# The low parts of the down-projection weights made by an accumulating DMA instead of by VectorE

## The chip, the cores and the metric

One core of one Trainium2 chip runs the whole program in one launch. The metric is the device time of that core in microseconds (us), lower is better. Times are medians of several executions; the profile is of one execution.

## What is computed

The reference is a decoder trunk of two layers in float32 on 256 tokens of width 1024. The part that matters here is the feed-forward block, which stands twice in every layer (four times in the run), before and after a group of token mixers:

```python
D_MODEL, SEQ, DEPTH, D_FF = 1024, 256, 2, 2816

def swiglu(x, w_up, w_down):
    g, u = jnp.split(x @ w_up, 2, axis=-1)
    return (jax.nn.silu(g) * u) @ w_down

for i in range(DEPTH):
    x = x + 0.5 * swiglu(rmsnorm(x, norm_ffn1[i]), w_ffn1_up[i], w_ffn1_down[i])
    ...
    x = x + 0.5 * swiglu(rmsnorm(x, norm_ffn2[i]), w_ffn2_up[i], w_ffn2_down[i])
    ...
```

The mixers (windowed attention, a gated recurrence, latent attention, each with its projections) and the per-layer embedding gate are left out here; the change does not touch them.

## The kernel before, in words

**Three products for one.** TensorE is fed float32r operands (a float32 rounded to fewer mantissa bits). To keep float32 accuracy, each operand is split into a rounded part h and a remainder l = value - h, and `mm3` (lines 205 to 209) adds three matmuls: h times h (L207), h times the low part of the moving operand (L208) and the low part of the stationary operand times h (L209). In the down projection the weights are the moving operand, so L208 is the matmul that reads a weight's l.

**Units.** Weights come in units of up to 128 partitions x 1024 elements (512 KB). `fetch` (lines 187 to 193) takes a `raw` tile and has SyncE (SP) load it from HBM. `split_unit` (lines 195 to 203) takes an `h` and an `l` tile, has ScalarE (ACT) write h as a rounding copy of raw (L201) and VectorE (DVE) write l = raw - h (L202). `unit` (lines 182 to 185) does both. There are 4 buffers for raw, 5 for h and 5 for l (line 1056); a buffer is taken again when all readers of its last content are done. So the load of a unit waits, at the head of SP's queue, for the DVE subtraction four units earlier, and the ACT copy of a unit waits for the matmuls of the unit five earlier. The whole run has 512 units; 88 of them, all 128x1024, are of the down projections.

**The feed-forward block** (`ffn`, lines 288 to 374) runs over 11 blocks of 256 hidden columns. Block b takes four up units, runs 16 matmul triples with them into two PSUM tiles (one for each half of the tokens), has ACT apply silu (L308) and DVE the product (L309), and then runs the down projection of the block before it, with two down units d0 and d1, each of 128 hidden rows x 1024 columns. In program order a block's units are thus u0, u1, u2, u3, d0, d1. In blocks 1 to 9 the up units are consumed one after the other, for both token halves; in the first and the last block token half by token half, so that there the four units come free only in the second pass.

**The last block** (lines 353 to 373) runs two down projections: d0 and d1 of block 9, then d0 and d1 of block 10, with the norm of the finished token half after them. Four down units are alive at once.

**Order on the engines.** The order of the instructions on each engine is laid down when the program is built and follows program order by priority, with waits on semaphores; each engine and each DMA queue takes its instructions in that order. GpSimd (POOL) has little to do: the power for the norms (L224), a product (L589), and two DMA issues at the start (L960, L971).

Of the kernel before, what the change touches and what calls it, by code (L numbers as in the profile page):

```python
# [9 lines left out]
F32R = mybir.dt.float32r  # L10
BF16 = mybir.dt.bfloat16
I32 = mybir.dt.int32
AF = mybir.ActivationFunctionType
OP = mybir.AluOpType
# [115 lines left out]
class Build:  # L130
# [51 lines left out]
    def unit(self, name, block, q):  # L182
        if (name, block, q) in self.early:
            return self.early.pop((name, block, q))
        return self.split_unit(*self.fetch(name, block, q))

    def fetch(self, name, block, q):
        nc = self.nc
        off, k, n = self.where[self.layer][name, block, q]
        m = k * n  # L190
        raw = self.wraw.tile([128, 1024], F32, name="raw")
        nc.sync.dma_start(raw[:, :m], self.a[f"weights{self.layer}"][off:off + 128 * m].rearrange("(p m) -> p m", p=128))
        return raw, k, n
# [908 lines left out]
```

## Time and profile before

| what | us |
|---|---|
| median of 2 runs | 1562.87 |
| the runs | 1562.22, 1563.51 |
| span of the profiled execution | 1560.1 |
| busy in it: PE, PEld, DVE, ACT, POOL | 1538.6, 1285.2, 940.4, 867.1, 36.4 |

PE is TensorE's matmuls, PEld its weight loads (they overlap), DVE is VectorE, ACT ScalarE, POOL GpSimd, SP SyncE. The span runs from the first to the last instruction of the profiled execution; the 2.8 us between it and the median is what lies around the span and the scatter of the runs. Matmuls are pipelined and their ends are modelled: a matmul of 512 columns is shown with some 0.39 us, but the next one starts about 0.23 us after it.

### The profile page before, as it was taken

The numbers are of one execution on the slowest core, as the hardware profiler recorded it, in microseconds if no ns is written. First come the engines' busy times: TensorE is split into PE (matmuls) and PEld (weight loads), VectorE is DVE, ScalarE is ACT, GpSimd is POOL, SyncE is SP. The second block draws the span as 40 slices with busy tenths as digits, with TensorE's granted clock in tenths as the row PEclk, the third lists the DMA queues.
The fourth block names the chain that finished last, engine by engine and source line by source line (L and its number), as shares of the span: only waits on it lengthen the run. The fifth ranks groups of instructions, "written<-read, shape, count | busy, mean of one in ns | idle before, by whom it ended". The sixth has DMA issues, their size and how long they took to land.

```text
span 1560.1 us, 20882 instructions
## 1 busy us (share of the span) xinstructions
PE 1538.6 (99%) x7896; PEld 1285.2 (82%) x7896; DVE 940.4 (60%) x1504; ACT 867.1 (56%) x1315; POOL 36.4 (2%) x48
## 2 busy tenths in 40 slices
PE   8999999999999999999999999999999999999997
PEld 6888888899878888888888888889998788888886
DVE  6555577567756665555765456675677466655456
ACT  6444486477564464444764445855875644644455
POOL 0000010000000000000000000100000000000000
PEclk9999999999999999999999999999999999999999
DMA  8555545343425555565565554544335355556652
GB/s 303 187 191 187 172 156 176 125 146 130 156 88 182 189 183 188 177 193 173 180 202 189 176 192 158 181 150 137 125 110 176 116 195 177 188 189 188 188 171 95
DMA packets 76469, 264.61 MB, mean 170 GB/s; under 512 B 8608, under 2 KB 9520, under 8 KB 76368
## 3 DMA queue, kind: packets, MB, share of 16 engines
q1 hardware_dynamic: 76144, 263.06, 51.5%
q8 instruction: 62, 1.02, 0.3%
q0 software_dynamic: 80, 0.16, 0.1%
q14 instruction: 39, 0.32, 0.1%
q10 hardware_dynamic: 144, 0.05, 0.0%
HBM read 262.19 MB, written 1.05 MB: 169 GB/s over the span
## 4 chain that ended last, share of the span: by engine, by line
PE 94%; ACT 2%; DVE 2%; DMA 1%; issue 1%; POOL 0%; SPq 0%; POOLq 0%; DVEq 0%; ACTq 0%
PE pu L207 21%; PE pu L209 21%; PE pu L208 21%; PE acc L207 5%; PE acc L208 5%; PE acc L209 5%; PE sq L209 2%; PE sq L208 2%; PE sq L207 2%; PE psa L497 1%; PE pt L314 1%; PE pt L234 1%; PE po L519 1%; PE psc L841 1%; DMA raw<-in_weights_dram 1%; PE psc L840 1%
## 5 line engine op out<-in xcount | busy, mean ns | idle before, releaser
L202 DVE TENSOR_TENSOR l<-raw,h 128x1024 fp32r<-128x1024 f32 (+3 forms) x512 | 599.9, 1185 | 399.2 <-ACT h L201 394.0
L201 ACT CAST h<-raw 128x1024 fp32r<-128x1024 f32 (+1 forms) x511 | 512.0, 1016 | 380.4 <-PE pu L209 236.6
L207 PE MATMUL pu<-h,xth 128*128 128x512 f32 (+3 forms) x1376 | 534.3, 389 | 7.1 <-DVE h L201 6.4
L208 PE MATMUL pu<-l,xth 128*128 128x512 f32 (+3 forms) x1376 | 525.5, 382 | 2.1 <-DVE l L202 2.1
L209 PE MATMUL pu<-h,xtl 128*128 128x512 f32 (+3 forms) x1376 | 524.5, 381 | 0.0
L207 PEld LDWEIGHTS pu<-h,xth 128*128 128x128 f32 x1376 | 259.4, 189 | 52.7 <-ACT xth L217 6.3
L208 PEld LDWEIGHTS pu<-l,xth 128*128 128x128 f32 x1376 | 259.6, 189 | 48.5 <-DVE l L202 4.8
L209 PEld LDWEIGHTS pu<-h,xtl 128*128 128x128 f32 x1376 | 259.1, 188 | 46.7 <-issue 1.3
L207 PE MATMUL acc<-h,fh 128*128 128x512 f32 x352 | 140.2, 398 | 0.0
L209 PE MATMUL acc<-h,fl 128*128 128x512 f32 x352 | 139.1, 395 | 0.0
L208 PE MATMUL acc<-l,fh 128*128 128x512 f32 x352 | 138.9, 395 | 0.0
L209 PEld LDWEIGHTS acc<-h,fl 128*128 128x128 f32 x352 | 66.3, 188 | 15.5
L208 PEld LDWEIGHTS acc<-l,fh 128*128 128x128 f32 x352 | 66.5, 189 | 15.0
L207 PEld LDWEIGHTS acc<-h,fh 128*128 128x128 f32 x352 | 66.3, 188 | 14.6
L308 ACT ACTIVATE sg<-pu,rstd 128x256 f32<-128x256 f32 x88 | 41.8, 475 | 64.3 <-PE pu L209 64.2
L309 DVE SCALAR_TENSOR_TENSOR hd<-pu,rstd,sg 128x256 f32<-128x256 f32 x88 | 42.3, 480 | 39.0 <-ACT sg L308 39.0
L207 PE MATMUL pu<-h,fh 128*128 128x512 f32 x128 | 51.3, 401 | 1.6 <-DVE merged L896 1.6
L208 PE MATMUL pu<-l,fh 128*128 128x512 f32 x128 | 51.0, 398 | 0.0
L209 PE MATMUL pu<-h,fl 128*128 128x512 f32 x128 | 50.8, 397 | 0.0
L207 PE MATMUL sq<-h,xth 128*128 128x512 f32 x128 | 50.4, 394 | 0.0
L209 PE MATMUL sq<-h,xtl 128*128 128x512 f32 x128 | 50.1, 391 | 0.0
L208 PE MATMUL sq<-l,xth 128*128 128x512 f32 x128 | 50.1, 391 | 0.0
(230 smaller groups left out, 1411.1 us busy)
## 6 DMA issues: line engine op xcount, KB each, us to landing
raw<-in_weights_dram SPq DMA_DIRECT2D x446, 512.0 KB, 4.2
raw<-in_weights_dram SPq DMA_DIRECT2D x48, 384.0 KB, 3.4
raw<-in_weights_dram SPq DMA_DIRECT2D x8, 320.0 KB, 3.1
raw<-in_weights_dram SPq DMA_DIRECT2D x8, 256.0 KB, 2.7
xin<-in_xt_dram SPq DMA_DIRECT2D x4, 256.0 KB, 6.2
x<-in_x_dram SPq DMA_DIRECT2D x2, 512.0 KB, 8.9
out_dram<-o SPq DMA_DIRECT2D x4, 256.0 KB, 2.1
cf<-in_const_f_dram SPq DMA_DIRECT2D x1, 928.0 KB, 8.3
```

The source lines that it names most:

```text
L201: (copy or nc.scalar.copy)(h[:, :m], raw[:, :m])
L202: nc.vector.tensor_tensor(l[:, :m], raw[:, :m], h[:, :m].bitcast(F32), op=OP.subtract)
L207: mm(out, ah, bh, start=start, stop=False)
L208: mm(out, ah, bl, start=False, stop=False)
L209: mm(out, al, bh, start=False, stop=stop)
L234: nc.tensor.transpose(pt[:, k, :], src[:, half * 512 + k * 128:half * 512 + (k + 1) * 128], self.ident)
L308: nc.scalar.activation(sg, pu[t][:, 0, :], AF.Silu, scale=rstd[t])
L309: nc.vector.scalar_tensor_tensor(hd, pu[t][:, 1, :], rstd[t], sg, op0=OP.mult, op1=OP.mult)
L314: nc.tensor.transpose(pt[:, f, t * 128:(t + 1) * 128], hd[:, f * 128:(f + 1) * 128], self.ident)
L497: mm(ps[:, g, :], self.aqk[r, h // 2, qt * 128:(qt + 1) * 128], self.aqk[r, 6 + h // 2, kb * 128:(kb + 1) * 128], start=True, stop=True)
L519: mm(po[:, qt, :], PTt[n][:, g, :], self.av[:, kb, h * 64:(h + 1) * 64], start=(g == 0 and n < 2), stop=(g == 2 and n != 1))
L840: mm(o, qnT[:, hd, qt * 128:(qt + 1) * 128], knT[:, hd, 0:128 * (qt + 1)], start=True, stop=False)
```

## The change

For units whose name ends in `_down`, l is made in another way. ACT first writes l as the rounded copy of -raw, which is -h, and then h as before; then GpSimd issues a DMA from raw onto l that adds raw to what is there. The result, raw - h, is the same. The DVE subtraction of these units is gone. All other units are as before.

```diff
     def unit(self, name, block, q):
         if (name, block, q) in self.early:
             return self.early.pop((name, block, q))
+        if name.endswith("_down"):
+            return self.split_unit_by_dma(*self.fetch(name, block, q))
         return self.split_unit(*self.fetch(name, block, q))
+
+    def split_unit_by_dma(self, raw, k, n):
+        nc = self.nc
+        m = k * n
+        h = self.wh.tile([128, 1024], F32R, name="h")
+        l = self.wl.tile([128, 1024], F32R, name="l")
+        nc.scalar.activation(l[:, :m], raw[:, :m], AF.Copy, scale=-1.0)
+        nc.scalar.copy(h[:, :m], raw[:, :m])
+        nc.gpsimd.dma_start(l[:, :m], raw[:, :m], accum_op=OP.add)
+        return Unit(h[:, :m].rearrange("p (k n) -> p k n", k=k), l[:, :m].rearrange("p (k n) -> p k n", k=k))
```

## Rows read from the trace of the kernel before

**Rows 1.** The page: busy time of each engine, and the chain that ended last.

```profile
PE 1538.6 (99%) x7896; PEld 1285.2 (82%) x7896; DVE 940.4 (60%) x1504; ACT 867.1 (56%) x1315; POOL 36.4 (2%) x48
...
PE 94%; ACT 2%; DVE 2%; DMA 1%; issue 1%; POOL 0%; SPq 0%; POOLq 0%; DVEq 0%; ACTq 0%
```

**Rows 2.** Whom PE waited for, whole run: us in total, times, longest us.

```profile
PE pu L207 <- DVE h L201: 6.4, 1, 6.4
PE pu L208 <- DVE l L202: 2.1, 6, 0.5
...
PE pu L209 <- DVE l L202: 0.6, 2, 0.3
```

**Rows 3.** Windows of one block's length: engines' busy time and count, clock, DMA share, GB/s.

```profile
107.00:124.00 17.00, 17.00 (x78) 13.99 (x77) 8.74 (x9) 7.59 (x10) 0.00 (x0) 1.00 0.54 186
124.00:141.00 17.00, 17.00 (x78) 13.96 (x77) 8.73 (x9) 7.59 (x10) 0.00 (x0) 1.00 0.57 183
```

**Rows 4.** Groups of instructions by line and shape: count, busy us, mean ns, idle before.

```profile
L202 DVE TENSOR_TENSOR l<-raw,h 128x1024 fp32r<-128x1024 f32 x446 | 542.1, 1228 | 382.6 <-ACT h L201 377.6
L201 ACT CAST h<-raw 128x1024 fp32r<-128x1024 f32 x445 | 461.7, 1050 | 367.2 <-PE pu L209 224.9 <-PE acc L209 124.9 <-DMA raw<-in_weights_dram 9.9
```

**Rows 5.** Timeline of ACT, middle block: start us, us; the idle before.

```profile
106.86 2.00 ACT L201 CAST h<-raw 128x1024 fp32r<-128x1024 f32 x2 [3.47 <-PE acc L209]
108.77 0.57 ACT L214 CAST fh<-pt 128x512 fp32r<-128x512 f32 x1
110.76 1.05 ACT L201 CAST h<-raw 128x1024 fp32r<-128x1024 f32 x1 [1.41 <-PE pu L209]
...
119.30 1.04 ACT L201 CAST h<-raw 128x1024 fp32r<-128x1024 f32 x1
123.80 2.00 ACT L201 CAST h<-raw 128x1024 fp32r<-128x1024 f32 x2 [3.47 <-PE acc L209]
```

**Rows 6.** Timeline of PE, same block: the first reads of d0's and d1's l.

```profile
118.96 0.40 PE L208 MATMUL acc<-l,fh 128*128 128x512 f32 x1
...
119.66 0.39 PE L208 MATMUL acc<-l,fh 128*128 128x512 f32 x1
```

**Rows 7.** Timeline of SP's DMA issues, same block.

```profile
110.33 0.33 SPq L192 DMA_DIRECT2D raw<-in_weights_dram  x1
...
113.10 0.33 SPq L192 DMA_DIRECT2D raw<-in_weights_dram  x1
```

**Rows 8.** Timeline of ACT and DVE, last block: block 9's d1, block 10's d0 and d1.

```profile
182.60 1.05 ACT L201 CAST h<-raw 128x1024 fp32r<-128x1024 f32 x1 [0.89 <-PE pu L209]
...
183.68 3.94 DVE L202 TENSOR_TENSOR l<-raw,h 128x1024 fp32r<-128x1024 f32 x3 [1.45 <-ACT h L201]
...
183.96 1.06 ACT L201 CAST h<-raw 128x1024 fp32r<-128x1024 f32 x1 [0.30 <-PE pu L209]
...
185.32 1.06 ACT L201 CAST h<-raw 128x1024 fp32r<-128x1024 f32 x1 [0.30 <-PE pu L209]
```

**Rows 9.** Timeline of PE, last block: first reads of those three units' l.

```profile
187.62 0.40 PE L208 MATMUL acc<-l,fh 128*128 128x512 f32 x1
...
189.93 0.39 PE L208 MATMUL acc<-l,fh 128*128 128x512 f32 x1
...
190.62 0.40 PE L208 MATMUL acc<-l,fh 128*128 128x512 f32 x1
```

**Rows 10.** DMA issues: queue, count, KB each, median us from issue to landing.

```profile
raw<-in_weights_dram SPq DMA_DIRECT2D x446, 512.0 KB, 4.2
...
raw<-in_weights_dram SPq DMA_DIRECT2D x8, 256.0 KB, 2.7
...
gnorm<-in_b_gnorm_dram POOLq DMA_DIRECT2D x1, 96.0 KB, 6.0
mask_b<-in_const_i_dram POOLq DMA_DIRECT2D x1, 64.0 KB, 4.6
ident<-in_const_f_dram SPq DMA_DIRECT2D x1, 64.0 KB, 8.7
```

**Rows 11.** Whom POOL waited for, whole run: us in total, times, longest us.

```profile
POOL rstd L224 <- DVE ms L223: 532.0, 13, 176.2
```

## The prediction

> **What bounds the kernel now.** I read the page first. PE is busy 1538.6 of 1560.1 us, and the chain that ended last is 94% PE, 2% ACT, 2% DVE [rows 1]. VectorE is at 60%, so to relieve it is worth something only where PE waits for it. The list of PE's waits says where: for DVE's l in all 2.1 us at L208 and 0.6 us at L209 [rows 2], at matmuls that write `pu`; no row has `acc`, the tile that the down projections write. (The 6.4 us are the start of the run.) A window of one feed-forward block shows the same from the other side: 17.00 of 17.00 us PE, but 8.74 DVE and 7.59 ACT, granted clock 1.00, DMA 0.54 to 0.57 [rows 3]. TensorE sets the pace, and the work on the weights runs some units ahead. What counts is how far ahead each l of a down unit is; I read that from the timeline of a middle block and of a last block.
>
> **Removed.** 88 DVE subtractions at 1.228 us, 108 us of DVE [rows 4]. PE waited for none of them, so I count nothing gained. In a middle block h of d1 starts at 110.76, so h and l are done 1.05 and 1.23 us later, at 113.04, and PE first reads that l at 119.66 [rows 4 to 6]: 6.6 us of cover. d0 has more.
>
> **Added on ACT.** 88 negating copies of 128x1024. No such copy is in the trace; I price it as the rounding copy of the same size, 1.05 us [rows 4] (it could hardly take less than that copy, and the most that I allow is the 1.23 us of the DVE pass over the same data). Two of them back to back take 2.00 us, so each next one starts 0.95 us later [rows 5]. A block gains 2.1 us on an engine that is busy 7.59 of 17.00 [rows 3], so as throughput it is free; as latency it stands in front of the DMA and of h. Behind a negating copy in ACT's queue stand h of the same unit, then fh (L214), then the next unit's. In a middle block fh runs at 108.77 and ACT is idle 1.41 us before 110.76 [rows 5]; it absorbs one copy, and fh is read only by the next down projection.
>
> **Added: the DMA.** This is the term that decides. Call L the time from the end of the negating copy until PE may read l: semaphore, GpSimd writing descriptors, transfer with its addition, landing. The trace has no accumulating DMA and none of POOL's of that size, so I bound it. Below: 4.2 us, what SP's loads of the same 512 KB take from issue to landing [rows 10]. From POOL there are two rows, 64 KB in 4.6 us and 96 KB in 6.0 us, both in the crowded opening, where an SP load of 64 KB took 8.7 us [rows 10]. From 256 to 512 KB SP's landing grows by 1.5 us, so 448 KB more are worth 2.6 us; 4.6 + 2.6 = 7.2 us. An addition must read l as well as raw: a DMA share of 0.55 over 17 us for six loads is 1.6 us of transfer per 512 KB [rows 3], so the second read makes it 8.8 us, and standing behind one load once makes it 10.4 us, my upper end. Against that stands that the POOL rows are inflated by the opening. I let the second read and that inflation cancel and take L = 7.0 us, nearest to the row of POOL's own queue; the ends 4.2 and 10.4 are kept for the range.
>
> The Trainium skill, in "Collectives: The Full Stack", section "The bandwidth ceiling", says that a reduce in the DMA engines runs at half the rate of a copy, since each output needs two reads through one ring while the add itself is free. No row here shows an accumulation; by that rule the sum would hold the 1.6 us in full, and L would be 8.6 instead of 7.0.
>
> **A middle block.** ACT starts u3's and d0's h at 106.86 and some 107.8, and d1's at 110.76, when u0's buffer comes free [rows 5]; the negating copies would start at these times. d0: 107.81 + 1.05 + 7.0 = 115.9, read at 118.96. d1: 110.76 + 1.05 + 7.0 = 118.81, read at 119.66 [rows 6]. Spare 0.85 us: no stall. PE would wait for d1 from L = 7.85 on, for d0 from 10.1 on. There are 36 such pairs (blocks 0 to 8 of four feed-forwards; the pattern of rows 5 and 6 repeats every 17 us, block 0's lead is a little shorter).
>
> The raw buffer is held until that DMA has read it, so the load four units on is late: d0's successor was issued at 110.33, d1's at 113.10 [rows 7]; now 115.9 and 118.8, and the loads queued behind them on SP with them. Their h's ran at 119.30 and 123.80 [rows 5], 9.0 and 10.7 us after the issue; less the landing of 4.2 us [rows 10], 4.8 and 6.5 us of that was waiting, against a delay of 5.6. The first h may come 0.8 us late; it belongs to the third up unit of the next block, and that block's up units begin only when the down projection has ended at 123.80 [rows 5]. Free at L = 7; where it crowds the next DMA it makes L longer, which the upper end holds.
>
> **The last block.** Here there are three down units in a row: h starts at 182.60, 183.96 and 185.32 [rows 8], PE reads their l at 187.62, 189.93 and 190.62 [rows 9]. Now ACT alternates negation and h at 0.95 us: negations start at 182.60, 184.50, 186.40 and end 1.05 us later. With L = 7.0 l is ready at 190.65, 192.55, 194.45. First stall: 190.65 - 187.62 = 3.03. Everything on PE moves by it: the second is read at 192.96, no stall; the third at 193.65, stall 0.80. Together 3.83 us, and nothing gives it back, since PE is the bound and the prefetch cannot run on while PE holds the buffers. Four such blocks: 15.3 us. With L = 4.2 it is 0.23 + 0.80, four times 1.03 = 4.1 us.
>
> **POOL's queue.** The DMAs are issued in order with the powers of the norms. Those wait for DVE's sums in any case [rows 11], and the last down unit of a feed-forward is issued before the norm that follows it. Nothing.
>
> **Sum.** 1560.1 - 0 + 15.3 = 1575.4 us of span; the median lies 2.8 above the span, so 1578.
>
> **The rivals.**
>
> *The wait moves into every block (slower).* From L = 7.85 on, PE stops for d1 in each of 36 blocks, and it does not fade: the buffers are released by PE, so the next block has the same lead. At L = 8.6: 0.75 x 36 = 27, last blocks 4 x (4.63 + 0.80) = 22, in all 49, 1612 us. At 10.4: 2.55 x 36 = 92 and 4 x 7.2 = 29, 1684 us. The line of 2% (31 us, about what a measurement can tell here from no change) is crossed at L = 8.2. For it: two reads, 0.55 of the DMA engines taken already. Against it: in a middle block SP's next load waits for this very DMA, so d0's has the engines nearly to itself.
>
> *As quick as an SP load.* With L = 4.2 or 5 the cost is 4 to 7 us, 1567 to 1570. For it: the loads of rows 10, themselves queued behind each other. Against: POOL took 4.6 us for an eighth of the bytes. The Trainium skill speaks for it ("DMA: Bandwidth & Descriptors", section "Anatomy of one DMA", fits a DMA from GpSimd with 2.0 us and the bytes at 436 GB/s, by which 512 KB would take an estimated 3.2 us and the change would cost nothing); the two POOL rows here disagree, with 4.6 and 6.0 us for far less.
>
> *VectorE's relief is worth something (faster).* All PE waits for l together are 2.7 us [rows 2], and none is at a down unit, so even if all went it would be 1560; not 2%.
>
> *Loads run dry.* Only with L beyond some 15 us: a raw buffer passes one down and two up units in two blocks (34 us), which leaves 34 - 18.5. No row speaks for that.
>
> **How the numbers follow.** Forecast, L between 5 and 8.2: 0.49, times 1570 to 1594. Rival in every block: 0.36. As quick as a load: 0.13. Faster: 0.02 (of it next to nothing beyond 2%, 0.01). That gives 0.01 faster, 0.63 within 2%, 0.36 slower. The range takes in the quick end and goes up into the first rival to L = 9.5 (59 + 25 us): 1563 to 1648.
>
> **What would show it.** Right: POOL has 88 DMA rows of 512 KB landing in 6 to 8 us; DVE falls by about 108 us and ACT rises by about 92; PE's waits show a new row at `acc` L208 for the DMA onto l, some 8 times, 3 us the longest, 15 us in all; the window of a middle block is still 17.0 us long with PE full. Wrong: that row 36 times more, and the blocks longer than 17 us (L over 7.85), or no such row at all (L under 4).

## The result and the profile after

The changed kernel took 1599.34 us (median of 2 runs, 1598.57 to 1600.1), the kernel before 1562.87: ratio 1.0232, 95% interval 1.0213 to 1.0251. It is slower by 36.5 us, where 15.3 were forecast. The profiled execution took 1598.57 us with a span of 1596.8, 36.7 more than before; its span is what the following divides up. In the table further down, one run of e_d0_only (1678.66 us, at a granted clock of 0.87) and one of the kernel before (3952.43 us) are left out as slow ones. Line numbers of the changed kernel are 12 higher from the old L186 on: the negating copy is L194, the rounding copy of a down unit L195, the DMA L196, the other roundings L213, VectorE's subtraction L214, the three products L219 to L221.

The page: busy times, two DMA queues (q1 carries SP's loads, q0 POOL's DMAs; packets, MB, share of the 16 DMA engines), and the issues.

```profile
PE 1552.5 (97%) x7896; PEld 1288.2 (81%) x7896; DVE 840.3 (53%) x1416; ACT 952.4 (60%) x1403; POOL 112.4 (7%) x136
...
q1 hardware_dynamic: 76144, 263.06, 50.3%
q0 software_dynamic: 12752, 46.31, 15.6%
...
raw<-in_weights_dram SPq DMA_DIRECT2D x446, 512.0 KB, 4.6
l<-raw POOLq DMA_DIRECT2D x88, 512.0 KB, 6.5
```

Against [rows 1], VectorE loses 100.1 us and ScalarE gains 85.3, much as forecast, and neither shows in the time. The new row is the DMA onto l: 88 times, 6.5 us from issue to landing. Whom PE waited for, whole run (us, times, longest):

```profile
PE acc L220 <- DMA l<-raw: 20.6, 18, 3.5
PE pu L219 <- DVE h L213: 6.2, 1, 6.2
PE pu L220 <- DVE l L214: 2.1, 6, 0.5
...
PE pu L221 <- DVE l L214: 0.6, 2, 0.3
```

The old waits stand as in [rows 2]; the first line is new. So PE stops for the DMA, 18 times where the forecast had 8, and not 36 times more as the rival in every block had it. The list names 20.6 of 36.7 us: nine waits in the last blocks, 15.4 us, and nine elsewhere, 5.2. To place the rest I took, for each of the 40 down projections, the end of its last product onto `acc`, subtracted the same in the kernel before, and then what had been lost up to there. That gives the loss block by block:

```
feed-forward  blocks 0 to 8 (first, second, ...)             last block
0             +3.4  0.0 +0.1 +0.1 +0.3 +0.5  0.0  0.0  0.0    +6.3
1             +0.1 +1.0  0.0  0.0  0.0  0.0  0.0  0.0 +0.4    +8.3
2             +0.5 +0.2  0.0  0.0  0.0 +0.3 +0.3 +0.4  0.0    +5.1
3             -0.6 +0.8 +0.3 +0.7  0.0 +0.1 +1.6  0.0  0.0    +5.2
```

The four last blocks lose 24.8 us, the 36 others 10.4 (a first block's number holds what lies before it, too), what follows the last feed-forward 1.4. The forecast had 15.3, 0 and 0. That the waits in the last blocks come so near to 15.3 is luck: the 24.8 us hold stretches at half the TensorE clock as well, shown below. The numbers are of one execution; with the same sixteen DMAs the last blocks of e_dma_last, e_neg_prio, e_fill and e_low_last lose 23.1 to 28.2. Now the last block of the first feed-forward: ScalarE's negations, the three DMAs on POOL, and PE.

```profile
186.73 1.06 ACT L194 ACTIVATE l<-raw 128x1024 fp32r<-128x1024 f32 x1 [0.66 <-PE pu L220]
187.69 1.03 ACT L195 CAST h<-raw 128x1024 fp32r<-128x1024 f32 x1
188.63 1.05 ACT L194 ACTIVATE l<-raw 128x1024 fp32r<-128x1024 f32 x1
189.59 1.03 ACT L195 CAST h<-raw 128x1024 fp32r<-128x1024 f32 x1
190.53 1.05 ACT L194 ACTIVATE l<-raw 128x1024 fp32r<-128x1024 f32 x1
```

```profile
188.08 0.87 POOL L196 DMA_DIRECT2D l<-raw  x1 [3.62 <-ACT l L194]
189.98 0.87 POOL L196 DMA_DIRECT2D l<-raw  x1 [1.02 <-ACT l L194]
191.87 0.87 POOL L196 DMA_DIRECT2D l<-raw  x1 [1.02 <-ACT l L194]
```

```profile
195.70 0.50 PE L220 MATMUL acc<-l,fh 128*128 128x512 f32 x1 [3.55 <-DMA l<-raw]
...
197.23 0.63 PE L220 MATMUL acc<-l,fh 128*128 128x512 f32 x1
...
201.35 0.50 PE L220 MATMUL acc<-l,fh 128*128 128x512 f32 x1 [0.59 <-DMA l<-raw]
```

The negations stand 1.90 us apart, as worked out from [rows 8]. From the end of the first (187.79) to PE's read at 195.70 it is 7.9 us; from the end of the third (191.58) to 201.35 it is 9.8. The forecast had 7.0 for each. In the four last blocks, from the end of the negation to the landing, the first of the three took 7.9, 5.8, 6.7 and 7.2 us, the third 9.7, 9.3, 8.6 and 8.7. Between the two stalls the matmuls run at 0.63 us where they took 0.39: the granted clock is at half. Windows of two middle blocks, and of that stretch (us, PE, PEld, DVE, ACT, POOL, clock, DMA share, GB/s):

```profile
107.00:124.00 17.00, 16.80 (x76) 13.48 (x75) 6.47 (x7) 9.53 (x11) 1.74 (x2) 1.00 0.91 248
124.00:141.00 17.00, 17.00 (x77) 13.96 (x78) 6.26 (x7) 9.59 (x11) 1.74 (x2) 1.00 0.90 259
...
197.20:200.60 3.40, 3.40 (x10) 2.29 (x8) 0.42 (x1) 0.37 (x1) 0.00 (x0) 0.51 1.01 267
```

The trace's clock stands at half for 3.4, 6.8, 3.4 and 3.4 us in the four last blocks, 17.1 in all.

The DMA share of a middle block went from 0.54 and 0.57 [rows 3] to 0.91 and 0.90. In the first of the two, ScalarE, POOL and PE did this:

```profile
112.52 1.05 ACT L195 CAST h<-raw 128x1024 fp32r<-128x1024 f32 x1 [0.24 <-DMA raw<-in_weights_dram]
113.47 0.58 ACT L226 CAST fh<-pt 128x512 fp32r<-128x512 f32 x1
113.95 2.01 ACT L194 ACTIVATE l<-raw 128x1024 fp32r<-128x1024 f32 x2
115.86 1.04 ACT L195 CAST h<-raw 128x1024 fp32r<-128x1024 f32 x1
```

```profile
115.30 1.81 POOL L196 DMA_DIRECT2D l<-raw  x2 [14.55 <-ACT l L194]
```

```profile
122.84 0.40 PE L220 MATMUL acc<-l,fh 128*128 128x512 f32 x1
...
123.90 0.50 PE L220 MATMUL acc<-l,fh 128*128 128x512 f32 x1 [0.20 <-DMA l<-raw]
```

In the source the negation comes before the rounding; the program puts d0's rounding and fh in front of it, and both negations together. The kernel runs 3.9 us late here (PE's first read of d0's l: 122.84 against 118.96 in [rows 6]), so the forecast's 108.86 for the end of d0's negation is 112.7 on this clock. It ended at 115.0, 2.3 us late: 0.8 because the rounding began late (0.24 of it waiting for d0's load), the rest by the place in the order. d1's negation ended at 115.96, 0.3 us later than forecast. d0's DMA goes out at 115.30, and d1's follows right behind it. By its packets in the trace d0's DMA moved from 116.76 to 119.78 and d1's from 119.46 to 123.55: one behind the other. d1's l took 7.9 us and PE waited 0.20 for it. Over the 36 middle blocks d1's l took 7.0 us in the median, as forecast, but 6.6 to 9.2, and the spare was 0.85.

### The profile page after: what moved, and what is told of

It reads as the page before. It is cut to its first block, busy times and chain, and to the rows that moved or that the text cites. A ratio compares the mean times of both kernels' runs of the same rounds, so it can differ in the third digit from the quotient of the medians.

```text
span 1596.8 us, 21137 instructions
## 1 busy us (share of the span) xinstructions
PE 1552.5 (97%) x7896; PEld 1288.2 (81%) x7896; DVE 840.3 (53%) x1416; ACT 952.4 (60%) x1403; POOL 112.4 (7%) x136
## 3 DMA queue, kind: packets, MB, share of 16 engines
q0 software_dynamic: 12752, 46.31, 15.6%
## 5 line engine op out<-in xcount | busy, mean ns | idle before, releaser
L214 DVE TENSOR_TENSOR l<-raw,h 128x1024 fp32r<-128x1024 f32 (+4 forms) x424 | 495.7, 1178 | 468.3 <-ACT h L213 464.7
L213 ACT CAST h<-raw 128x1024 fp32r<-128x1024 f32 (+3 forms) x423 | 423.2, 1009 | 308.0 <-PE pu L221 138.6
L219 PE MATMUL pu<-h,xth 128*128 128x512 f32 (+3 forms) x1376 | 534.4, 389 | 7.6 <-DVE h L213 6.2
L221 PE MATMUL pu<-h,xtl 128*128 128x512 f32 (+3 forms) x1376 | 524.2, 382 | 0.0
L219 PEld LDWEIGHTS pu<-h,xth 128*128 128x128 f32 x1376 | 259.4, 189 | 53.3 <-ACT xth L229 6.1
L221 PEld LDWEIGHTS pu<-h,xtl 128*128 128x128 f32 x1376 | 259.1, 188 | 46.8 <-issue 1.3
L220 PE MATMUL acc<-l,fh 128*128 128x512 f32 x352 | 144.4, 410 | 20.9 <-DMA l<-raw 20.6
L219 PE MATMUL acc<-h,fh 128*128 128x512 f32 x352 | 141.8, 405 | 0.0
L221 PE MATMUL acc<-h,fl 128*128 128x512 f32 x352 | 141.2, 401 | 0.0
L196 POOL DMA_DIRECT2D l<-raw x88 | 76.0, 863 | 617.3 <-ACT l L194 451.2
L195 ACT CAST h<-raw 128x1024 fp32r<-128x1024 f32 x88 | 91.7, 1042 | 8.7 <-DMA raw<-in_weights_dram 8.6
L194 ACT ACTIVATE l<-raw 128x1024 fp32r<-128x1024 f32 x88 | 90.6, 1057 | 5.3 <-PE pu L220 5.0
L221 PEld LDWEIGHTS acc<-h,fl 128*128 128x128 f32 x352 | 67.9, 193 | 14.9
L219 PEld LDWEIGHTS acc<-h,fh 128*128 128x128 f32 x352 | 67.5, 192 | 15.0
L227 DVE TENSOR_TENSOR fl<-pt,fh 128x512 fp32r<-128x512 f32 (+1 forms) x62 | 37.1, 603 | 36.7 <-ACT fh L226 36.7
L219 PE MATMUL pu<-h,fh 128*128 128x512 f32 x128 | 51.3, 401 | 1.6 <-DVE merged L908 1.6
L229 ACT ACTIVATE xth<-pt,gains 128x128 fp32r<-128x128 f32 x112 | 37.3, 366 | 23.3 <-PE pt L246 12.1
```

The costliest lines, as they stand in the source:

```text
L194: nc.scalar.activation(l[:, :m], raw[:, :m], AF.Copy, scale=-1.0)
L195: nc.scalar.copy(h[:, :m], raw[:, :m])
L196: nc.gpsimd.dma_start(l[:, :m], raw[:, :m], accum_op=OP.add)
L213: (copy or nc.scalar.copy)(h[:, :m], raw[:, :m])
L214: nc.vector.tensor_tensor(l[:, :m], raw[:, :m], h[:, :m].bitcast(F32), op=OP.subtract)
L219: mm(out, ah, bh, start=start, stop=False)
```

## The experiments

Three theories. A: what counts is the time L from the negation to the landed l against the lead of each unit, so the loss sits at PE's reads of l. B: 88 accumulating DMAs and the raw buffers that they hold slow the weights everywhere. C: the 88 copies and their order on ScalarE cost the time. Later ones, on the last block: D, the third DMA queues behind the two before it; E, the first wait and the half clock make the loss; F, the weight loads of the next units compete with the additions. The table is worked out like the blocks above (last blocks, other 36 and what lies between feed-forwards, the rest; us); ratios are against the kernel before on the same chip. The three columns of us are of one execution each.

| run | last | others | rest | median us | ratio [95%] |
|---|---|---|---|---|---|
| e_dve_add | 0.0 | 0.6 | 0.0 | 1562.47 | 1.0003 [0.9994, 1.0012] |
| e_dve_last | 0.0 | 8.9 | 0.3 | 1568.79 | 1.0045 [1.0033, 1.0058] |
| e_dma_last | 24.6 | 0.6 | -0.5 | 1586.42 | 1.0158 [1.0144, 1.0172] |
| e_copy | 9.4 | 1.6 | 3.6 | 1574.66 | 1.0085 [1.0071, 1.0098] |
| e_shadow | 0.0 | 8.9 | 7.3 | 1578.04 | 1.0109 [1.0095, 1.0122] |
| e_neg_prio | 23.1 | 6.2 | 1.7 | 1592.88 | 1.0196 [1.0182, 1.0210] |
| e_low_last | 28.2 | 3.7 | 1.5 | 1595.19 | 1.0210 [1.0196, 1.0224] |
| e_fill | 26.3 | 5.8 | 2.2 | 1597.36 | 1.0223 [1.0209, 1.0237] |
| e_tail3 | 12.6 | 5.9 | 1.1 | 1582.63 | 1.0135 [1.0119, 1.0151] |
| e_d0_only | 18.6 | 1.2 | 0.0 | 1582.19 | 1.0135 [1.0119, 1.0151] |
| e_d1_only | 21.6 | 2.2 | 0.0 | 1586.84 | 1.0159 [1.0145, 1.0174] |
| e_d0_short | 0.3 | 5.1 | 0.0 | 1565.54 | 1.0023 [1.0013, 1.0033] |
| e_short | 13.0 | 6.5 | 1.4 | 1583.76 | 1.0138 [1.0123, 1.0153] |
| e_combo | -0.1 | 0.6 | -0.5 | 1561.84 | 1.0000 [0.9991, 1.0008] |

**The copies on ScalarE alone.** The negating copy stays; VectorE adds onto it.

```diff
-        nc.gpsimd.dma_start(l[:, :m], raw[:, :m], accum_op=OP.add)
+        nc.vector.tensor_tensor(l[:, :m], raw[:, :m], l[:, :m].bitcast(F32), op=OP.add)
```

> The negating copy on ScalarE stays, but VectorE adds raw to it instead of the DMA. Theory A: l is ready 2.3 us after the negation starts, as before the change, and ScalarE has room: 1562 to 1567 us. Theory C (the 88 added copies on ScalarE and the order that they force there are what costs): most of the loss stays, 1585 us or more.

1562.47 us and no block late. 88 more copies on ScalarE cost nothing; as the only cause, C is out. What the DMA brings is all that is lost.

**Which blocks.** The DMA in blocks 0 to 8 only (e_dve_last, 72 of them; the first of the added lines), and in the last two only (e_dma_last, 16; the second):

```diff
-        if name.endswith("_down"):
+        if name.endswith("_down") and block < FB - 2:
+        if name.endswith("_down") and block >= FB - 2:
```

> The eight down units of blocks 9 and 10 of each feed-forward pair (four per feed-forward, 16 in all) are made by VectorE again, the other 72 stay with the DMA. Theory A (the time L until l is ready, against the lead of each unit): the loss sits in the last blocks, where the changed kernel lost 24.8 of its 36.7 us, so 1570 to 1578 us. Theory B (the DMA traffic and the raw buffers that it holds slow the weights everywhere): 72 of 88 DMAs are left and with them some 80% of the loss, about 1593 us.

> The mirror image: the DMA only for the 16 down units of blocks 9 and 10, VectorE for the other 72. Theory A: the last blocks lose what they lost, 20 to 27 us, 1583 to 1590 us, and the middle blocks are as long as before. Theory B: 16 of 88 DMAs, some 7 us, about 1570 us.

Both speak for A (the first lies 1.2 us under A's range). Sixteen of the 88 DMAs make 24.6 us, all of the last blocks' loss, and the other 72 make 9.1.

**What the addition costs.** The same DMA without the addition, so that l is raw itself (the remainder is not formed):

```diff
-        nc.gpsimd.dma_start(l[:, :m], raw[:, :m], accum_op=OP.add)
+        nc.gpsimd.dma_start(l[:, :m], raw[:, :m])
```

> The DMA copies raw onto l without adding (so l is raw instead of the remainder; the sum of the products is another one). It reads once instead of twice. Theory A with the second read as a full transfer: a packet of 4 KB falls from 0.34 us to about 0.17, landing from 6.5 to about 5.1 us, the first wait of each last block by 1.4 us and most waits of the middle blocks go: 1580 to 1588 us. If the landing is set by GpSimd's writing of descriptors and by fixed steps instead: landing 6.3 us or more, 1597 us or more.

1574.66, better than any theory said. Its queue and issue rows on the page:

```profile
q0 software_dynamic: 12752, 46.31, 8.2%
...
l<-raw POOLq DMA_DIRECT2D x88, 512.0 KB, 3.7
```

The same bytes take 8.2% of 16 engines where they took 15.6%: 1574.7 x 0.082 / 88 = 1.5 us of transfer for each against 1596.8 x 0.156 / 88 = 2.8. The landing is 3.7 us instead of 6.5. The addition nearly doubles the transfer, by 1.4 us, where the forecast put 1.6 for the second read. The landing grows by 2.8. Between the quickest landings, 2.9 us here and 4.5 in the changed kernel, are 1.6 us; the rest I take to be queueing, which these rows alone don't show. The Trainium skill ("Collectives: The Full Stack", section "The bandwidth ceiling") gives a reduce half the rate of a copy because it reads twice; these two rows agree.

**The traffic alone.** VectorE makes l; the negation and the accumulating DMA go into a scratch tile that nobody reads.

```diff
+        nc.vector.tensor_tensor(l[:, :m], raw[:, :m], h[:, :m].bitcast(F32), op=OP.subtract)
+        s = self.sh[:, self.shn % 3, :]
...
+        nc.scalar.activation(s[:, :m], h[:, :m], AF.Copy, scale=-1.0)
+        nc.gpsimd.dma_start(s[:, :m], raw[:, :m], accum_op=OP.add)
```

> VectorE makes l of all down units as before the change; beside it the same 88 negating copies and the same 88 accumulating DMAs go into a tile of their own that nobody reads (three slots in turn, in memory that the feed-forward leaves free), with raw held by them as in the changed kernel. Theory A (latency on the way to PE): almost nothing left, 1562 to 1569 us. Theory B (traffic and held raw buffers): most of the loss stays, 1585 us or more.

Within the feed-forwards 0.0 in every block, the last ones too, with all 88 DMAs running (a first block's number holds what lies before it): there A holds and B falls. But the time missed both forecasts, 1578.04: some 6 to 7 us are lost after each of the second and the fourth feed-forward, none of it at an l. The chain that ended last shows at what:

```profile
749.38 6.64 DMA pin<-in_p_dram
756.04 0.63 ACT fh L229
756.71 0.79 PE pu L222
757.51 0.43 PE pu L223
```

`pin`, the input of the next stage, was issued at 749.38, where the kernel before issued it at 742.83, and took 6.64 us. PE waited for it, and then ran at half clock (0.43 us from matmul to matmul in place of 0.23). So the traffic can delay a load that has little lead, on SP behind the weights. In the changed kernel no such loss is seen at that place; B is no part of its 36.7 us that I can show.

**The order on ScalarE, and the middle blocks.** The negation and its DMA are given priority (e_neg_prio); or in each down projection the products with h come first and those with l last (e_low_last), which gives l some 1.6 us more.

```diff
-        nc.scalar.activation(l[:, :m], raw[:, :m], AF.Copy, scale=-1.0)
+        with self.tc.high_priority(offset=200):
+            nc.scalar.activation(l[:, :m], raw[:, :m], AF.Copy, scale=-1.0)
+            nc.gpsimd.dma_start(l[:, :m], raw[:, :m], accum_op=OP.add)
         nc.scalar.copy(h[:, :m], raw[:, :m])
-        nc.gpsimd.dma_start(l[:, :m], raw[:, :m], accum_op=OP.add)
```

> The changed kernel with the negating copies and their DMAs given a higher priority when the order is laid down. On ScalarE d0's negation now stands before fh and d1's after it, where both stood behind fh, so that d0's DMA starts 0.5 us earlier and the two overlap less. Theory A with the order on ScalarE as a part of the middle blocks' loss: 2 to 8 us less than the changed kernel, 1591 to 1597 us; the last blocks keep theirs. If the middle blocks wait only for late raw loads: no change, 1598 to 1600 us.

> The changed kernel with the order of the down projection's matmuls changed: for each token half first all eight products with h (both halves of the columns), then the four with l. The first read of d1's l comes 1.15 us later in PE's order, of d0's 1.6 us later; everything else is as it was. Theory A: the waits of the middle blocks (up to 1.6 us) go nearly all, some 9 us, and each last block gains 1 to 3 us: 1580 to 1588 us. Theory B or C: no change, 1597 to 1601 us.

The priority put d0's negation in front of fh, not of the rounding. The other blocks' loss is 6.2 us with it, but four more runs with those blocks as in the changed kernel (e_dve_last, e_fill, e_tail3, e_short) lose 5.8 to 8.9 there: against 5.8 to 10.4, an effect of the order is not shown. With the later reads it is 3.7, under all of them, and one wait is left outside the last blocks, where the changed kernel has nine: there it is a matter of a microsecond or two of lead.

The time of e_low_last, 1595.19, missed A's range, for the last blocks keep 28.2. All waits of the run, and PE in its first last block:

```profile
PE acc L316 <- DMA l<-raw: 17.7, 7, 3.8
...
199.98 1.65 PE L316 MATMUL acc<-l,fh 128*128 128x512 f32 x3 [3.75 <-DMA l<-raw]
...
198.80:205.50 6.70, 5.52 (x17) 4.56 (x18) 2.66 (x7) 2.32 (x7) 0.56 (x1) 0.50 0.67 232
```

The later reads gather this block's waits into one of 3.75 us at the third l, and the half clock that sets in during it lasts 6.8 us. It does so in all four last blocks, 27.3 us in all against 17.1 in the changed kernel, and no further wait covers it. By these rows the slow matmuls take back what the later reads gain; no run was made of it.

**The half clock.** 22 products on a zero tile, just where PE waits in the last block, keep it busy (work added; `dummy` is read by nobody):

```diff
...
+                        for n in range(22):
+                            nc.tensor.matmul(dummy, self.zero[:, 0:128], self.zero, start=True, stop=True)
```

> The changed kernel with 22 matmuls of zeros (384 columns, into a PSUM tile that nobody reads) put before the first wait of each last block, at block 9's d1, so that PE is busy through most of that wait. Theory A with the clock as a term of its own (in the changed kernel each last block is followed by 3.4 or 6.8 us at half the clock, 8.5 us of work in all): the wait stays as long, but the stretch at half clock behind it goes in most of the four places: 1590 to 1596 us. If the clock costs nothing of its own: as the changed kernel or longer by what the zeros overrun, 1599 to 1604 us.

```profile
190.60 3.75 PE L313 MATMUL dummy<-zero 128*128 128x384 bf16 x22
...
199.30 0.50 PE L220 MATMUL acc<-l,fh 128*128 128x512 f32 x1 [1.70 <-DMA l<-raw]
...
190.50:200.60 10.10, 8.40 (x45) 5.74 (x44) 3.00 (x5) 2.80 (x5) 0.87 (x1) 1.00 1.03 247
```

The clock holds 1.00 through the stretch, but the third unit's wait grows from 0.59 to 1.70 us and the block loses 5.6 in place of 6.3. Of the other three only one has a stretch at half clock, 3.4 us, and yet the four lose 26.3 us, no less than before; 1597.36 lies between the two forecasts. With three DMAs the slow matmuls lie in the shadow of the third landing, so E falls as the main cause here. One stretch of the changed kernel does not: in the second feed-forward 5.7 of the 6.8 us at half clock come after the third landing, and that block lost the most, 8.3.

**The last block: other additions, or loads?** VectorE takes the last unit of each feed-forward (e_tail3), or the DMA makes only each block's first unit (e_d0_only) or only its second (e_d1_only); one added line for each, in this order:

```diff
-        if name.endswith("_down"):
+        if name.endswith("_down") and (block, q) != (FB - 1, 1):
+        if name.endswith("_down") and q == 0:
+        if name.endswith("_down") and q == 1:
```

> As the changed kernel, but the last unit of each feed-forward (block 10's d1) is made by VectorE, so that two DMAs follow each other in the last block instead of three. Theory D (the third DMA, queued behind the other two and behind loads, sets the end of a last block; the first wait and the half clock lie within its shadow): each last block loses some 4 us instead of 5 to 8, 1589 to 1593 us. Theory E (the first wait and the half clock behind it make the loss): no change, 1597 to 1601 us.

> Only the first unit of each pair goes by the DMA (44 of 88), the second by VectorE, so that in a middle block no accumulating DMA follows another at once. Theory D (a DMA by itself lands some 5.1 us after its issue; what makes 6.5 to 9 of it is the one before): middle blocks lose nothing, each last block about 1 us, 1563 to 1569 us. If a DMA by itself takes 6.5 us: each last block 2 to 3 us, 1569 to 1575 us.

> The mirror image: only the second unit of each pair goes by the DMA. Its lead is the shorter one (7.85 us in a middle block, 3.97 us in block 9). Theory D: landing 5.1 to 5.6 us, middle blocks lose nothing, each last block 1.5 to 2.5 us, 1567 to 1575 us. If it is the number of DMAs and not their following each other: half the loss of the changed kernel, 1579 to 1583 us.

Without the third DMA half of the loss goes, more than D had forecast, but the single ones missed: 18.6 and 21.6 us in the last blocks, with hardly another addition near (in e_d0_only the one before has landed 1.8 us before the next is issued). (They don't add up to 24.8 because a stall moves all later reads, so one covers the other.) D cannot be all. PE in the first last block of e_d0_only, a window behind its wait, and the DMA queues from 187.7 to 191.0 there:

```profile
194.52 0.79 PE L220 MATMUL acc<-l,fh 128*128 128x512 f32 x1 [2.73 <-DMA l<-raw]
195.12 0.63 PE L221 MATMUL acc<-h,fl 128*128 128x512 f32 x1
...
194.50:200.60 6.10, 6.08 (x16) 4.88 (x17) 1.38 (x2) 0.85 (x3) 0.00 (x0) 0.50 0.45 153
...
q1 hardware_dynamic: 154, 0.52, 59.1%
q0 software_dynamic: 46, 0.19, 29.3%
```

The DMA was issued at 186.78, yet in these 3.3 us the weight loads (q1) took two thirds of the DMA engines' busy time. A wait of 2.73 us, and then 6.1 us at half clock, which nothing hides here (some 3 us lost), are this block's 5.7. So the half clock counts where a single wait stands. Then the loads were tried: of the four units after each feed-forward only a sixteenth of the columns is loaded, and their copies read it repeatedly.

```diff
                 d1 = down_units(b)
+                self.cut = 4
...
+        self.short = m // 16 if self.cut > 0 else m
+        self.cut -= 1
+        nc.sync.dma_start(raw[:, :self.short], self.a[f"weights{self.layer}"][off:off + 128 * m].rearrange("(p m) -> p m", p=128)[:, :self.short])
...
+        src = raw[:, :m] if c == m else raw[:, None, :c].to_broadcast([128, m // c, c])
```

> Only the first unit of each block is made by the accumulating DMA (as in the run with the first unit alone), and of the four weight units that follow each feed-forward only a sixteenth of the columns is loaded, which their two copies spread over the whole unit (so the products with these units are of other numbers). If the loads that are released in a last block slow the addition, the lone DMA there takes about 2.7 us from its first packet to its last instead of 4.3, starts a microsecond sooner, and each of the four last blocks loses about 2 us less: 1574 to 1578 us, against 1583.5 with whole loads. If the loads have no part in it, the DMA keeps its 4.3 us and the time is 1581 to 1584 us.

> The changed kernel with the same four units after each feed-forward loaded to a sixteenth. If the loads of the next units share the blame for the third addition of a last block (landing 9.2 to 9.7 us after its negation began), its landing falls to 7.5 to 8.2 us and each last block loses 1.5 to 2.5 us less: 1589 to 1593 us. If the other two additions alone are to blame, the landing stays and the time is 1597 to 1600 us.

F is right, by more than was expected: with one addition the last blocks' 18.6 us go to 0.3; with all three, 24.8 to 13.0. The same 2.2 us (189.5 to 191.7) of the last block in the changed kernel, where the first of the three additions was issued at 188.08:

```profile
q1 hardware_dynamic: 92, 0.38, 73.9%
```

and in e_short, where it was issued at 188.40:

```profile
q0 software_dynamic: 96, 0.39, 93.7%
```

Each row is the only queue that moved anything. With whole loads the addition has moved nothing until 191.7: its first packet starts 3.67 us after the issue, against 1.44 in e_short. The one load beside it, and what SP's loads wait for in the whole run:

```profile
188.41 0.33 SPq L204 DMA_DIRECT2D raw<-in_weights_dram  x1
...
SPq L204 <- DMA l<-raw: 391.4, 88, 8.5
```

Each of the 88 additions holds its raw buffer, and SP's next load waits for it. The load at 188.41 went out 0.05 us after the addition before (block 9's d0) had landed, at 188.36, and stood in the way of the next one; the load after it went out at 195.71, when that one had landed, beside the third. PE's waits in that block of e_short:

```profile
193.05 0.50 PE L226 MATMUL acc<-l,fh 128*128 128x512 f32 x1 [0.58 <-DMA l<-raw]
...
195.94 0.50 PE L226 MATMUL acc<-l,fh 128*128 128x512 f32 x1 [0.31 <-DMA l<-raw]
...
198.76 0.51 PE L226 MATMUL acc<-l,fh 128*128 128x512 f32 x1 [1.62 <-DMA l<-raw]
```

The reads are 2.8 to 2.9 us apart, the transfer of one addition: D is the rest, three additions one behind the other. From the ends of the negations (188.10 and 191.89) L is 5.0 us for the first and 6.9 for the third, and no stretch at half clock follows these waits.

**Nothing of it left.** The DMA in blocks 1 to 8 only, with the priority for the negation and the products with l last:

```diff
-        if name.endswith("_down"):
+        if name.endswith("_down") and 0 < block < FB - 2:
...
```

> The DMA only where the lead is longest: blocks 1 to 8 of each feed-forward (64 of 88 units), VectorE for blocks 0, 9 and 10; with the priority for the negating copies, and with the products with l last in each token half of the down projection. Theories A and D: hardly a wait is left, and since PE is the bound there is no gain either: 1562 to 1566 us. Theory B: 64 of 88 DMAs still cost 1580 us or more.

1561.84, the time of before: where the lead holds, 64 accumulating DMAs are free, and they bring nothing. No run was faster than the kernel before.

## Why the prediction was wrong

Right were the mechanism and its places. PE is the bound, VectorE's relief is worth 0 (e_combo: VectorE at 56%, the same time), the copies on ScalarE are free (e_dve_add), and the last block's three units in a row lose first. The rival in every block did not come: the 36 blocks lose 10.4 us in all, not 0.75 us or more each. The quick rival's L of 5 us is right for an addition that has nothing in its way (5.0 in e_short), but its 1567 to 1570 us did not come: in the kernel a load or another addition stands there. The estimate of 3.2 us by the fit in the Trainium skill ("DMA: Bandwidth & Descriptors", section "Anatomy of one DMA") comes near the 3.7 us that the plain copy took, not near the 6.5 of the addition.

Two terms of the sum failed, and a small third was missing: 36.7 - 15.3 = 21.4 us, of which 9.5 are the last blocks, 10.4 the others and 1.4 the stretch after them.

*"Four such blocks: 15.3 us"* measured 24.8. The step that failed is the one L of 7.0 us for three additions in a row. For the first of the three it was right, 5.8 to 7.9 and 6.9 on average; the third took 8.6 to 9.7, 9.1 on average. The forecast's own sum comes to L - 3.17 us for a block by the third unit (187.45 + L against the read at 190.62), so 9.1 in place of 7.0 makes it 23.6 us for the four, and the half clock behind the third landing in one block can make the rest. Two things make the third late. The additions stand one behind the other: by the forecast's own numbers an addition moves for 3.2 us and the next follows after 1.90, so the queue was there to be seen; in e_short, without loads, L is 5.0, 5.9 and 6.9. And the loads stand between them: without them the four blocks lose 13.0, so the loads, with the half clock that goes with them, are 11.8 of the 24.8. That 13.0 is near the forecast is luck: its 7.0 came from POOL's two rows and a second read that were let cancel, while the 6.9 of e_short is 5.0 and two waits in line.

The upper end of 10.4 had "standing behind one load once"; it was taken for the improbable end, on the argument that SP's next load waits for this very DMA. The loads do wait so, all 88 times. But the load that one addition lets go then stands beside the next addition. The kernel before shows the loads that are due at this place, in a window of its last block from 187 to 195 us:

```profile
q1 hardware_dynamic: 500, 1.66, 63.0%
```

That is 5 us of transfer; the changed kernel spreads it between the additions. I had taken the DMA share from the middle block alone [rows 3].

*"Spare 0.85 us: no stall"* for a middle block measured 10.4 us over 36 blocks. The step took one value where the landing scatters: d1's l took 7.0 us in the median and more than 7.85 in six of the 36. In the block shown, its DMA stood behind d0's, which the forecast had some 3 us ahead of it; d0's negation came late by its place in the order and, to a smaller part, because its rounding began late. Shown is that a little more lead takes most of the loss (e_low_last, e_combo) and that a plain copy leaves 1.6 us; how much the order and the late loads have in it stays open. Of what remains in e_neg_prio, e_low_last and e_copy, 1 to 4.5 us sit in the first two blocks of the first feed-forward; their cause was not tried.

The half clock after a stall was not forecast. In the changed kernel it lay mostly in the shadow of the third landing; where a single wait stood it cost some 3 us (the block of e_d0_only), and by the trace it took back the gain of e_low_last.

## What to carry to other kernels

A DMA that takes work over from an engine that is not the bound is priced by its landing against the lead of the reader, at the place with the least lead, and with the queues as they are there: read the DMA share of that very stretch, and ask which loads the same event releases. The buffer that one such DMA frees brings a load into the way of the next. If several such DMAs follow each other, each waits for the one before, so the last of the row has the longest landing. And the order in the source is not the order on the engine: a new instruction in front of a DMA is to be costed with the place that the program may give it, or pinned.

## What was not expected of the hardware

An accumulating DMA of 512 KB between two tiles held all 16 engines for 2.8 us, a copy for 1.5. Its issue kept POOL for 0.86 us. Several in line hardly overlapped: the first packets of the three in the last block are 2.6 and 2.5 us apart (191.75, 194.38, 196.88), though they were issued 1.9 us apart. And an idle PE of 3.55 us was followed by 3.4 us at a granted clock of 0.51, the 1.2 GHz level, while in the same block of e_fill, without that gap, it stayed at 1.00.
